# A conditioned convolution block on one core: conditioning and gate computed along the free axis of VectorE

## Chip, core and metric

One core of a Trainium2 chip. The metric is the device time of one execution, in microseconds (us). Three runs of the kernel before took 1729.15, 1729.73 and 1729.89 us; the median is 1729.73.

## What is computed

The block is a decoder layer (width 4096, 256 tokens, batch 1, all f32), cut here to what matters:

```
mod   = silu(c) @ W_ada + b_ada            # c: 4096 values; W_ada: 4096 x 12288
shift, scale, gate = split(mod, 3)         # 4096 values each
h     = rmsnorm(x, norm_g) * (1 + scale) + shift
P     = h @ W_in                           # 4096 x 14336
y_A   = a_b * conv3(a_c * a_x) * silu(a_z)             # mixer A, 2048 channels
y_B   = silu(LN(conv31(b_v * sigmoid(b_g)))) * silu(b_z)  # mixer B, 2048 channels
x     = x + gate * ([y_A, y_B] @ W_out)    # 4096 x 4096
out   = rmsnorm(x, final_g)
```

`W_ada` is 201 MB of the 517 MB that are read: two thirds of it (shift and scale) must be worked out before the rows of `W_in` that they belong to, one third (gate) is needed only in the output projection.

## The kernel before, in words

**Products.** TensorE works through *steps*. A step is one 512 KB load of weights (two contraction tiles of 128 rows by 512 columns): ScalarE rounds it to a high part `w_h` (line 143), VectorE subtracts to get the low part `w_l` (line 144), and TensorE runs 12 products of 512 columns (lines 156 to 158: two contraction tiles, two token tiles, three pairs of parts). `SEGS` (line 59) orders 448 steps of the input projection in six blocks of the contraction (4, 4, 4, 6, 6 and 8 tiles); within a block all 28 column tiles pass, and at the end of each (a *segment*) VectorE adds the PSUM tile to `acc` (line 469). The output projection takes 128 more steps, numbers 448 to 575. The last block begins at step 336.

**Conditioning.** `cact` holds silu(c) with contraction rows on the partitions. Shift and scale of a group of two or four tiles (`mod_steps`, line 176) come from 16 or 32 loads of 512 KB; VectorE multiplies each row of weights by its own scalar and adds it to an accumulator `modacc` (`ada_cols`, line 170), 512 or 1024 columns wide. At the end TensorE sums `modacc` over the partitions with products of one column (line 197), VectorE adds the bias (line 200) and forms `gscT` (line 201). `make_h` (line 255) then scales `x.T` and splits it into `hT`, which the products need.

**Gate.** Four pieces of 1024 columns, 32 loads each (`gate_steps`, line 207). Pieces 0 and 1 run on TensorE, four narrow products side by side per two loads (`step_t`, line 223, products at line 231); pieces 2 and 3 on VectorE (`step_v`, line 218). Each ends in products with a matrix of ones (line 248) that sum over the partitions and leave the gate in all of them. `GATE_RUN` (line 39) spreads the pieces over steps 0 to 70, 70 to 115, 115 to 185 and 185 to 231 counted from step 336.

**Order.** Background work stands in a queue with due steps; `next_w` (line 431) loads and splits the weights of the next step, then runs what is due (`run_due`). The framework's scheduler then fixes one order per engine. All the loads named here go through SP's queue in order, and all of them share the pool `raws` of 10 buffers (line 94): a load goes out when a buffer is free. The parts `w_h` and `w_l` have three buffers each.

**Work of mixer B.** From about step 355 to step 491 the width-31 convolution runs beside the products: per tap four multiplications on ScalarE (line 370) and one addition on VectorE (line 371), 120 taps in all; then a layernorm.

**Start.** `x_stats` (line 274) loads `x.T` in eight pieces and sums squares with products against ones (line 290), while the first 16 loads of conditioning arrive.

Of the kernel before, what the change touches and what calls it, by code (L numbers as in the profile page):

```python
# [55 lines left out]
PK = O_LNB + NB  # L56
# [23 lines left out]
UNITS = [[0, KD]]   # contraction tiles conditioned together: the first, their number  # L80
for _k in range(KD, KT, KD):
    if UNITS[1:] and UNITS[-1][1] == KD and FIRST_USE[_k] - FIRST_USE[_k - KD] < 4:
        UNITS[-1][1] += KD
    else:
        UNITS.append([_k, KD])


@with_exitstack
def decoder_block(ctx: ExitStack, tc: tile.TileContext, x, c, w_mod, w_gate, w_in, w_out, xt, pk, b_gate, final_g, out):
# [3 lines left out]
    ada = ctx.enter_context(tc.tile_pool(name="ada", bufs=1))  # L93
    raws = ctx.enter_context(tc.tile_pool(name="raws", bufs=10))
# [13 lines left out]
    # ---------------- constants and small parameters  # L108
# [38 lines left out]
    def products(ps, act, parts, k0, first, last, tokens=range(NS)):  # L147
        """act[k // 2][:, k % 2, hi/lo, s] is stationary; ps [P, NS, CT]."""
# [11 lines left out]
    def split_act(dst, src):  # L160
        """dst [P, 2, hi/lo, S] <- src [P, 2, S]"""
# [3 lines left out]
    # ---------------- conditioning: silu(c) @ w_ada, 1024 columns at a time  # L165
    modT = const.tile([P, 64], F32, name="modT")
    gscT = const.tile([P, KT], F32, name="gscT")
    hT = {}

    def ada_cols(acc, raw, j):  # L170
        if j == 0:
            nc.vector.tensor_scalar(out=acc, in0=raw, scalar1=cact[:, 0:1], scalar2=None, op0=ALU.mult)
        else:
            nc.vector.scalar_tensor_tensor(out=acc, in0=raw, scalar=cact[:, j:j + 1], in1=acc, op0=ALU.mult, op1=ALU.add)  # L174

    def mod_steps(k0, n):
        """Shift and scale of contraction tiles k0 .. k0 + n."""
        state = {}

        m = 4 // n      # contraction rows per load  # L180
        at = UNITS.index([k0, n])
        first_load = sum(KT * u // 4 for _, u in UNITS[:at])

        def step(j):
            raw = rawt(f"mod{k0}_{j}", (P, m, n * 256))
            nc.sync.dma_start(raw, w_mod[first_load + j // m].rearrange("p (m c) -> p m c", m=m))
            if j == 0:
                state["acc"] = ada.tile([P, n * 256], F32, tag="acc", name=f"modacc{k0}")
            for i in range(m):
                ada_cols(state["acc"], raw[:, i], j + i)  # L190

        def finish():
            acc = state["acc"].rearrange("p (q t c) -> p q t c", t=2, c=256)
            ps = misc(f"modps{k0}", (P, 2, n))
# [3 lines left out]
            for t in range(2):  # L198
                col = 32 * t + k0
                nc.vector.tensor_tensor(out=modT[:, col:col + n], in0=ps[:, t], in1=pks[:, O_BADA + col:O_BADA + col + n], op=ALU.add)  # L200
            nc.vector.scalar_tensor_tensor(out=gscT[:, k0:k0 + n], in0=modT[:, 32 + k0:32 + k0 + n], scalar=1.0, in1=pks[:, O_G + k0:O_G + k0 + n], op0=ALU.add, op1=ALU.mult)

        return [lambda j=j: step(j) for j in range(0, KT, m)] + [finish]
# [70 lines left out]
    def x_stats():  # L274
        """1 / rms of the rows of x, in all partitions"""
        ps = misc("x_ps", (P, S))
        for ci in range(8):
# [355 lines left out]
```

## Time and profile before

| | |
|---|---|
| three runs | 1729.15, 1729.73, 1729.89 us (median 1729.73) |
| span of the profiled execution | 1728.9 us, 21319 instructions |
| TensorE (PE) busy | 1669.5 us, 97% |
| weight loads (PEld), overlapping PE | 1340.1 us, 78% |
| VectorE (DVE) busy | 1506.9 us, 87% |
| ScalarE (ACT) busy | 937.0 us, 54% |
| GpSimd (POOL) busy | 2.9 us |
| DMA | 522.42 MB, mean 302 GB/s, 85.8% of 16 engines for SP's queue |

The span runs from the first to the last instruction of one profiled execution. Its own device time is not given apart from the span; the median of the runs is 0.8 us above the span, and that is what lies around it. Busy times are shares of the whole span and average over stages with different limits; the stages are the start (to 101 us, step 16), the first five blocks (101 to 988 us, steps 16 to 336), the last block with the output projection of mixer A (988 to 1535 us, steps 336 to 512) and the rest.

### The profile page before, as it was taken

To read this page: it belongs to the slowest core of one execution; us is meant where nothing else is said; L and a number is where in the kernel's file an instruction comes from. 1 tells how busy PE (TensorE), PEld (TensorE's weight loads), DVE (VectorE), ACT (ScalarE), POOL (GpSimd) and SP (SyncE) were. 2 spreads that over 40 slices of the span, in tenths; PEclk is the share of its full clock that TensorE was granted. 3 is DMA by queue.
4 is the path that set the end of the run, shared out by engine and by line. 5 is a ranking of instruction groups with operands and counts; after the bars stand their busy time and mean duration, and the time that the engine had idled before them with its cause. 6 is when DMAs were issued, how large, how long until landed. Compare 5 with 4: busy or idle time off the path is not lost.

```text
span 1728.9 us, 21319 instructions
## 1 busy us (share of the span) xinstructions
PE 1669.5 (97%) x7480; PEld 1340.1 (78%) x7480; DVE 1506.9 (87%) x1490; ACT 937.0 (54%) x1304; POOL 2.9 (0%) x10
## 2 busy tenths in 40 slices
PE   2899999999999999999999999999999999999997
PEld 1778788888888888888888877777777887878885
DVE  7887998899898988898898857898998999989996
ACT  3555443443334333343333468888887888564443
POOL 0000000000000000000000000000000000000000
PEclk8899999999999999999999999999999999999998
DMA  9899899999999998999899977766888888779993
GB/s 387 327 317 331 300 344 327 325 320 332 310 335 326 330 326 302 312 352 329 292 340 321 327 243 248 253 230 232 288 278 281 277 286 280 266 254 335 361 345 116
DMA packets 145715, 522.42 MB, mean 302 GB/s; under 512 B 16196, under 2 KB 16196, under 8 KB 145608
## 3 DMA queue, kind: packets, MB, share of 16 engines
q1 hardware_dynamic: 145464, 520.71, 85.8%
q8 instruction: 58, 0.95, 0.2%
q10 hardware_dynamic: 144, 0.35, 0.1%
q14 instruction: 49, 0.40, 0.1%
HBM read 516.81 MB, written 4.19 MB: 301 GB/s over the span
## 4 chain that ended last, share of the span: by engine, by line
PE 86%; DVE 6%; DMA 4%; issue 3%; ACT 1%; SPq 0%; DVEq 0%; ACTq 0%
PE ps L156 23%; PE ps L157 23%; PE ps L158 23%; PE pb L158 3%; PE pb L156 3%; PE pb L157 3%; DVE w_l L144 2%; PE gateps L231 2%; DMA gate<-in_w_gate 2%; DVE cv L371 1%; PE pa L157 1%; PE pa L158 1%; DVE modacc L174 1%; PE pa L156 1%; DMA mod<-in_w_mod 1%
## 5 line engine op out<-in xcount | busy, mean ns | idle before, releaser
L143 ACT CAST w_h<-w_r 128x1024 fp32r<-128x1024 f32 x576 | 603.7, 1052 | 654.2 <-PE ps L158 490.4
L144 DVE TENSOR_TENSOR w_l<-w_r,w_h 128x1024 fp32r<-128x1024 f32 x576 | 700.8, 1220 | 118.8 <-ACT w_h L143 113.2
L156 PE MATMUL ps<-w_h,hT 128*128 128x512 f32 x1792 | 705.8, 394 | 3.0 <-ACT hT L162 2.6
L157 PE MATMUL ps<-w_l,hT 128*128 128x512 f32 x1792 | 700.7, 391 | 5.6 <-DVE w_l L144 5.6
L158 PE MATMUL ps<-w_h,hT 128*128 128x512 f32 x1792 | 699.4, 390 | 0.0
L156 PEld LDWEIGHTS ps<-w_h,hT 128*128 128x128 f32 x1792 | 337.5, 188 | 96.8 <-issue 10.8
L157 PEld LDWEIGHTS ps<-w_l,hT 128*128 128x128 f32 x1792 | 337.5, 188 | 79.9 <-DVE w_l L144 10.9
L158 PEld LDWEIGHTS ps<-w_h,hT 128*128 128x128 f32 x1792 | 337.3, 188 | 70.6
L174 DVE SCALAR_TENSOR_TENSOR modacc<-mod,cact,modacc 128x512 f32<-128x512 f32 (+1 forms) x341 | 337.4, 990 | 4.6 <-DMA mod<-in_w_mod 1.5
L370 ACT ACTIVATE pr<-uT,pks 128x255 f32<-128x255 f32 (+14 forms) x480 | 198.1, 487 | 2.1 <-DVE cv L371 1.6
L469 DVE TENSOR_TENSOR acc<-ps,acc 128x1024 f32<-128x1024 f32 x135 | 164.9, 1221 | 22.9 <-PE ps L158 22.4
L371 DVE TENSOR_TENSOR cv<-cv,pr 128x1020 f32<-128x1020 f32 (+14 forms) x120 | 138.7, 1156 | 27.1 <-ACT pr L370 26.4
L157 PE MATMUL pa<-w_l,yT 128*128 128x512 f32 x256 | 100.6, 393 | 2.4 <-DVE w_l L144 2.4
L156 PE MATMUL pa<-w_h,yT 128*128 128x512 f32 x256 | 100.1, 391 | 0.0
L156 PE MATMUL pb<-w_h,yT 128*128 128x512 f32 x256 | 100.1, 391 | 0.0
L158 PE MATMUL pb<-w_h,yT 128*128 128x512 f32 x256 | 100.0, 391 | 0.0
L158 PE MATMUL pa<-w_h,yT 128*128 128x512 f32 x256 | 100.0, 390 | 0.0
L157 PE MATMUL pb<-w_l,yT 128*128 128x512 f32 x256 | 99.6, 389 | 0.0
L174 DVE SCALAR_TENSOR_TENSOR gateacc<-gate,cact,gateacc 128x1024 f32<-128x1024 f32 x62 | 79.4, 1280 | 5.8 <-DMA gate<-in_w_gate 5.6
L157 PEld LDWEIGHTS pa<-w_l,yT 128*128 128x128 f32 x256 | 48.0, 188 | 14.6 <-DVE w_l L144 4.8
L467 ACT COPY acc<-ps 128x1024 f32<-128x1024 f32 x28 | 28.5, 1017 | 51.7 <-PE ps L158 51.7
L156 PEld LDWEIGHTS pb<-w_h,yT 128*128 128x128 f32 x256 | 48.1, 188 | 10.3 <-ACT w_h L143 0.2
(129 smaller groups left out, 645.2 us busy)
## 6 DMA issues: line engine op xcount, KB each, us to landing
w_r<-in_w_in SPq DMA_DIRECT2D x448, 512.0 KB, 5.2
mod<-in_w_mod SPq DMA_DIRECT2D x256, 512.0 KB, 5.1
gate<-in_w_gate SPq DMA_DIRECT2D x128, 512.0 KB, 4.8
w_r<-in_w_out SPq DMA_DIRECT2D x128, 512.0 KB, 5.1
xs<-in_xt SPq DMA_DIRECT2D x8, 512.0 KB, 10.2
xr<-in_x SPq DMA_DIRECT2D x8, 512.0 KB, 7.0
out<-o SPq DMA_DIRECT2D x16, 256.0 KB, 2.7
xc<-in_xt SPq DMA_DIRECT2D x4, 512.0 KB, 5.2
```

What stands on the lines that cost most here:

```text
L143: nc.scalar.copy(hi, raw)
L144: nc.vector.tensor_tensor(out=lo, in0=raw, in1=hi.bitcast(F32), op=ALU.subtract)
L156: nc.tensor.matmul(out, ah, hi[:, i], start=f, stop=False)
L157: nc.tensor.matmul(out, ah, lo[:, i], start=False, stop=False)
L158: nc.tensor.matmul(out, al, hi[:, i], start=False, stop=l)
L174: nc.vector.scalar_tensor_tensor(out=acc, in0=raw, scalar=cact[:, j:j + 1], in1=acc, op0=ALU.mult, op1=ALU.add)
L231: nc.tensor.matmul(state["ps"][r:r + 1, 0], cact[:, j + i:j + i + 1], raws_[i][:, h * CT:(h + 1) * CT], start=j == 0, stop=j == KT - 2)
L370: nc.scalar.activation(out=pr[:, j, sh:], in_=u[:, j, :S - sh], func=AF.Copy, scale=cbw[:, 4 * i + j, TAPS - 1 - sh:TAPS - sh])
L371: nc.vector.tensor_tensor(out=o[:, :, sh:], in0=o[:, :, sh:], in1=pr[:, :, sh:], op=ALU.add)
L467: nc.scalar.copy(acc[e], ps)
L469: nc.vector.tensor_tensor(out=acc[e], in0=ps, in1=acc[e], op=ALU.add)
```

## The change

The layout of `W_ada` is turned: one *output column* per partition, the contraction along the free axis. silu(c) then has to stand in all partitions: `broadcast_c` loads c in four rows of 1024, TensorE copies each to 128 partitions (two products with one contraction row each), ScalarE applies silu into `cB` (128 x 4096). One `tensor_tensor_reduce` on VectorE multiplies a load of 128 columns by 1024 contraction rows with `cB` and sums along the free axis, starting from the bias or from the sum before; four of them make 128 columns. In the engine's order it is two instructions: the sum of products (128x1024) and one that writes the sum (128x1). Shift and scale are thereby done without TensorE; the unit of work is one tile, 8 loads and 8 such pairs, and `gscT`. All of the gate, 128 loads, is done the same way on VectorE, over steps 0 to 170 from step 336; the 4096 gate values are then transposed, written to DRAM and read back into all partitions, 1024 columns at a time, where the final weights are loaded. The loads keep their number and size (384 of 512 KB). `raws` has 7 buffers in place of 10 (`cB` takes 16 KB of each partition). `x_stats` now adds all eight pieces on VectorE before four products, and is called before the first conditioning; the weights of the first two steps are loaded ahead of the last four pieces of first work. The due steps of shift and scale follow the same rule, for one tile at a time.

```diff
-GATE_PE = (0, 1)    # gate columns (1024 each) worked out on TensorE, the others on VectorE
-GATE_RUN = {0: (0, 70), 1: (70, 115), 2: (115, 185), 3: (185, 231)}  # when, in steps from the last block on
+ROW = 1024
+GATE_RUN = (0, 170)
...
-    raws = ctx.enter_context(tc.tile_pool(name="raws", bufs=10))
+    raws = ctx.enter_context(tc.tile_pool(name="raws", bufs=7))
...
-    def ada_cols(acc, raw, j):
-        if j == 0:
-            nc.vector.tensor_scalar(out=acc, in0=raw, scalar1=cact[:, 0:1], scalar2=None, op0=ALU.mult)
-        else:
-            nc.vector.scalar_tensor_tensor(out=acc, in0=raw, scalar=cact[:, j:j + 1], in1=acc, op0=ALU.mult, op1=ALU.add)
+    def broadcast_c():
+
+        for q in range(D // ROW):
+            row = bigt(f"crow{q}", (P, ROW))
+            nc.sync.dma_start(row[:1], c[:, q * ROW:(q + 1) * ROW])
+            ps = pmm.tile([P, NS, CT], F32, tag="ps", name=f"cps{q}")
+            for h in range(2):
+                nc.tensor.matmul(ps[:, h], ones[:1], row[:1, h * CT:(h + 1) * CT], start=True, stop=True)
+            nc.scalar.activation(out=cB[:, q * ROW:(q + 1) * ROW], in_=ps, func=AF.Silu)
+
+    def ada_steps(name, srcs, bias, dst):
...
+        def step(q):
+            raw = rawt(f"{name}_{q}", (P, ROW))
+            nc.sync.dma_start(raw, srcs[q])
+            if q == 0:
+                state["part"] = part.tile([P, 4], F32, tag="part", name=f"part{name}")
+            p = state["part"]
+            nc.vector.tensor_tensor_reduce(out=raw, in0=raw, in1=cB[:, q * ROW:(q + 1) * ROW], scale=1.0, scalar=p[:, q - 1:q] if q else bias, op0=ALU.mult, op1=ALU.add, accum_out=dst if q == D // ROW - 1 else p[:, q:q + 1])
...
-            for t in range(2):
-                for i in range(n):
-                    nc.tensor.matmul(ps[:, t, i:i + 1], acc[:, i // 2, t, (i % 2) * P:(i % 2 + 1) * P], ones[:, 0:1], start=True, stop=True)
...
-                    nc.tensor.matmul(state["ps"][r:r + 1, 0], cact[:, j + i:j + i + 1], raws_[i][:, h * CT:(h + 1) * CT], start=j == 0, stop=j == KT - 2)
...
+    def gate_finish():
+
+        ps = misc("gate_ps", (P, P))
+        nc.tensor.transpose(ps[:KT], gateT, ident)
+        row = rawt("gate_row", (P, P))
+        nc.scalar.copy(row[:KT], ps[:KT])
+        nc.sync.dma_start(gate_d.rearrange("(k p) -> k p", p=P), row[:KT])
+
+    def gate_steps():
+        work = [f for k in range(KT) for f in ada_steps(f"gate{k}", w_gate[k], pks[:, O_BGATE + k:O_BGATE + k + 1], gateT[:, k:k + 1])]
+        return work + [gate_finish]
...
+    broadcast_c()
+    rstd = x_stats()
+    first_steps = [f for k in range(KD) for f in mod_steps(k)]
+    for f in first_steps[:-4]:
         f()
-    rstd = x_stats()
-    for f in first_steps[2:]:
+    load_ahead(AHEAD)
+    for f in first_steps[-4:]:
         f()
...
+    spread(gate_steps(), start_last + GATE_RUN[0], start_last + GATE_RUN[1])
...
+            t = gate[dt // 2] = bigt(f"gate{dt // 2}", (P, 1024))
+            nc.sync.dma_start(t, gate_d[dt * CT:dt * CT + 1024].partition_broadcast(P))
```

Two places of the order move as follows. The first is VectorE's queue in the last block, from the split of step 356 to that of step 358 (names carry buffer numbers; `w356_l` is the low part of step 356's weights, `cv0` and `pr0` are the convolution's sum and one tap's products, `acc18` a segment's sum). Before:

```order
L144 TENSOR_TENSOR w356_l_8088<-w356_r_8085,w356_h_8087 128x1024
L371 TENSOR_TENSOR cv0_7779<-cv0_7779,pr0_7_8011 128x4x249
L144 TENSOR_TENSOR w357_l_8108<-w357_r_8105,w357_h_8107 128x1024
L469 TENSOR_TENSOR acc18_1112<-ps24_18_8004,acc18_1112 128x1024
L371 TENSOR_TENSOR cv0_7779<-cv0_7779,pr0_8_8035 128x4x248
L144 TENSOR_TENSOR w358_l_8132<-w358_r_8129,w358_h_8131 128x1024
```

Now:

```order
L138 TENSOR_TENSOR w356_l_8000<-w356_r_7997,w356_h_7999 128x1024
L186 ISA gate4_0_8003,partgate4_8005<-gate4_0_8003,cB_95,pks_90 128x1024
L186 ISA partgate4_8005 128x1
L348 TENSOR_TENSOR cv0_7689<-cv0_7689,pr0_8_7952 128x4x248
L437 TENSOR_TENSOR acc18_1073<-ps24_18_7918,acc18_1073 128x1024
L138 TENSOR_TENSOR w357_l_8024<-w357_r_8021,w357_h_8023 128x1024
L348 TENSOR_TENSOR cv0_7689<-cv0_7689,pr0_9_7979 128x4x247
L186 ISA gate4_1_8033,partgate4_8005<-gate4_1_8033,cB_95,partgate4_8005 128x1024
L186 ISA partgate4_8005 128x1
L138 TENSOR_TENSOR w358_l_8051<-w358_r_8048,w358_h_8050 128x1024
```

Two pairs of the gate (rows of L186) stand between the splits of two steps, where before only the convolution and the segment's sum stood; the gate's products of that time were in TensorE's queue.

The second is SP's queue at the end of the gate, in the layernorm of mixer B (`w504_r` is the load of step 504's weights, `gate31_3` the last load of the gate, `gate_d` the write of the gate to DRAM). Before:

```order
L138 DMA w503_r_12044<-in_w_out 128x1024
L215 DMA gate2_25_12050<-in_w_gate 128x1024
L138 DMA w504_r_12070<-in_w_out 128x1024
L138 DMA w505_r_12109<-in_w_out 128x1024
L215 DMA gate2_26_12115<-in_w_gate 128x1024
L138 DMA w506_r_12130<-in_w_out 128x1024
```

Now:

```order
L182 DMA gate31_3_11992<-in_w_gate 128x1024
L132 DMA w503_r_12007<-in_w_out 128x1024
L132 DMA w504_r_12035<-in_w_out 128x1024
L210 DMA gate_d_96<-gate_row_12020 32x128
L132 DMA w505_r_12074<-in_w_out 128x1024
L132 DMA w506_r_12092<-in_w_out 128x1024
```

The write of the gate stands ahead of the load for step 505. It needs the last pair on VectorE, then a transpose on TensorE that stands behind the products of the layernorm's variance, then a copy on ScalarE.

## Rows read from the trace of the kernel before

**Rows 1.** The page: the chain that ended last, by engine, then by line.

```profile
PE 86%; DVE 6%; DMA 4%; issue 3%; ACT 1%; SPq 0%; DVEq 0%; ACTq 0%
PE ps L156 23%; PE ps L157 23%; PE ps L158 23%; PE pb L158 3%; PE pb L156 3%; PE pb L157 3%; DVE w_l L144 2%; PE gateps L231 2%; DMA gate<-in_w_gate 2%; DVE cv L371 1%; PE pa L157 1%; PE pa L158 1%; DVE modacc L174 1%; PE pa L156 1%; DMA mod<-in_w_mod 1%
```

**Rows 2.** Busy time of each engine by stage of the span (columns in the first row).

```profile
core 0: us, PE busy (x) PEld busy (x) DVE busy (x) ACT busy (x) POOL busy (x), PEclk, DMA share, GB/s
0.00:101.00 101.00, 60.09 (x230) 47.60 (x231) 79.98 (x109) 46.23 (x51) 0.99 (x8) 0.85 0.94 354
101.00:988.00 887.00, 883.83 (x3937) 729.15 (x3937) 790.82 (x757) 369.39 (x371) 0.00 (x0) 1.00 0.92 323
988.00:1535.00 547.00, 544.28 (x2523) 414.95 (x2522) 473.02 (x463) 434.60 (x772) 1.91 (x2) 1.00 0.77 261
1535.00:1728.90 193.90, 181.30 (x795) 148.41 (x793) 163.03 (x163) 86.78 (x113) 0.00 (x0) 0.97 0.81 296
```

**Rows 3.** Groups of VectorE instructions in the stretch 988 to 1535 us.

```profile
L174 DVE SCALAR_TENSOR_TENSOR gateacc<-gate,cact,gateacc 128x1024 f32<-128x1024 f32 x30 | 38.4, 1281 | 5.7 <-DMA gate<-in_w_gate 5.6
...
L172 DVE TENSOR_SCALAR gateacc<-gate,cact 128x1024 f32<-128x1024 f32 x1 | 0.7, 747 | 0.0
```

**Rows 4.** Groups of the whole span by shape: costs that the sums use.

```profile
L174 DVE SCALAR_TENSOR_TENSOR modacc<-mod,cact,modacc 128x1024 f32<-128x1024 f32 x155 | 198.3, 1279 | 0.1
...
L231 PE MATMUL gateps<-gate,cact 128*1 128x512 f32 x256 | 36.3, 591 | 0.0
...
L248 PE MATMUL gatesum<-gateacc,ones 128*128 128x512 f32 x16 | 7.5, 592 | 0.0
...
L172 DVE TENSOR_SCALAR modacc<-mod,cact 128x1024 f32<-128x1024 f32 x5 | 3.7, 747 | 0.0
...
L524 ACT ACTIVATION_READ_ACCUMULATOR xr<-o 128x1 f32 x14 | 2.6, 185 | 0.0
```

**Rows 5.** VectorE's timeline around 611, 1430 and 1719 us.

```profile
610.72 1.28 DVE L174 SCALAR_TENSOR_TENSOR modacc<-mod,cact,modacc 128x1024 f32<-128x1024 f32 x1
611.91 1.22 DVE L469 TENSOR_TENSOR acc<-ps,acc 128x1024 f32<-128x1024 f32 x1
...
1430.03 2.35 DVE L144 TENSOR_TENSOR w_l<-w_r,w_h 128x1024 fp32r<-128x1024 f32 x2
...
1719.34 0.15 DVE L585 TENSOR_SCALAR o_v<-o_v 128x1 f32<-128x1 f32 x1
```

**Rows 6.** Timeline of the start: first conditioning, a statistics product, first product.

```profile
5.53 0.49 DVE L172 TENSOR_SCALAR modacc<-mod,cact 128x512 f32<-128x512 f32 x1 [5.53 <-DMA mod<-in_w_mod]
...
22.36 3.56 PE L290 MATMUL x_ps<-xq,ones 128*128 128x256 f32 x8 [3.83 <-DVE xq L288]
...
50.78 0.79 PE L156 MATMUL ps<-w_h,hT 128*128 128x512 f32 x1 [2.62 <-ACT hT L162]
```

**Rows 7.** Busy time in 43.2 us of the middle, sixteen steps (columns as in Rows 2).

```profile
388.80:432.00 43.20, 43.20 (x192) 35.79 (x191) 41.56 (x36) 16.57 (x17) 0.00 (x0) 1.00 0.95 332
```

**Rows 8.** TensorE's conditioning products in the stretch 101 to 988 us.

```profile
L197 PE MATMUL modps<-ones,modacc 128*128 128x1 f32 x96 | 11.1, 243 | 0.0
```

**Rows 9.** VectorE's conditioning in the same stretch.

```profile
L174 DVE SCALAR_TENSOR_TENSOR modacc<-mod,cact,modacc 128x1024 f32<-128x1024 f32 (+1 forms) x276 | 288.8, 1046 | 1.8
...
L172 DVE TENSOR_SCALAR modacc<-mod,cact 128x1024 f32<-128x1024 f32 (+1 forms) x8 | 5.2, 647 | 0.0
```

**Rows 10.** DMA issues: bytes of each, median us from issue to landing.

```profile
w_r<-in_w_in SPq DMA_DIRECT2D x448, 512.0 KB, 5.2
```

**Rows 11.** Two stretches where TensorE paused (columns as in Rows 2).

```profile
190.00:213.00 23.00, 20.96 (x88) 15.69 (x87) 23.00 (x27) 7.34 (x7) 0.00 (x0) 1.00 0.81 264
86.40:129.60 43.20, 40.66 (x174) 32.49 (x173) 34.60 (x43) 22.30 (x24) 0.00 (x0) 0.96 0.91 317
```

**Rows 12.** TensorE's timeline just after its first product.

```profile
51.37 0.63 PE L157 MATMUL ps<-w_l,hT 128*128 128x512 f32 x1
51.80 0.63 PE L156 MATMUL ps<-w_h,hT 128*128 128x512 f32 x1
```

More of the change, by code (lines that the diff above doesn't have):

```diff
@@ L55 @@
 O_LNB = O_LNG + NB
-PK = O_LNB + NB
+O_BGATE = O_LNB + NB
+PK = O_BGATE + KT
 def _segments():
@@ L79, with decoder_block @@
     FIRST_USE.setdefault(_k, _t)
[L80 to L83, printed above, removed]
-    else:
-        UNITS.append([_k, KD])
 @with_exitstack
-def decoder_block(ctx: ExitStack, tc: tile.TileContext, x, c, w_mod, w_gate, w_in, w_out, xt, pk, b_gate, final_g, out):
+def decoder_block(ctx: ExitStack, tc: tile.TileContext, x, c, w_mod, w_gate, w_in, w_out, xt, pk, final_g, out):
     nc = tc.nc
@@ L92, in decoder_block @@
     big = ctx.enter_context(tc.tile_pool(name="big", bufs=33))
-    ada = ctx.enter_context(tc.tile_pool(name="ada", bufs=1))
-    raws = ctx.enter_context(tc.tile_pool(name="raws", bufs=10))
+    cbc = ctx.enter_context(tc.tile_pool(name="cbc", bufs=1))
+    part = ctx.enter_context(tc.tile_pool(name="part", bufs=4))
+    dram = ctx.enter_context(tc.tile_pool(name="dram", bufs=1, space=bass.MemoryType.DRAM))
+    raws = ctx.enter_context(tc.tile_pool(name="raws", bufs=7))
     split = ctx.enter_context(tc.tile_pool(name="split", bufs=3))
@@ L167, in decoder_block @@
     gscT = const.tile([P, KT], F32, name="gscT")
+    gateT = const.tile([P, KT], F32, name="gateT")
+    cB = cbc.tile([P, D], F32, name="cB")
     hT = {}
-    def ada_cols(acc, raw, j):
-        if j == 0:
-            nc.vector.tensor_scalar(out=acc, in0=raw, scalar1=cact[:, 0:1], scalar2=None, op0=ALU.mult)
-        else:
-            nc.vector.scalar_tensor_tensor(out=acc, in0=raw, scalar=cact[:, j:j + 1], in1=acc, op0=ALU.mult, op1=ALU.add)
-    def mod_steps(k0, n):
-        state = {}
[L180 to L190, printed above, removed]
-        def finish():
-            acc = state["acc"].rearrange("p (q t c) -> p q t c", t=2, c=256)
-            ps = misc(f"modps{k0}", (P, 2, n))
-            for t in range(2):
-                for i in range(n):
-                    nc.tensor.matmul(ps[:, t, i:i + 1], acc[:, i // 2, t, (i % 2) * P:(i % 2 + 1) * P], ones[:, 0:1], start=True, stop=True)
[L198 to L203, printed above, removed]
@@ new lines, in broadcast_c @@
+    def broadcast_c():
[7 more added lines that the diff above has]
+    def ada_steps(name, srcs, bias, dst):
+        state = {}
+        def step(q):
[5 more added lines that the diff above has]
+            nc.vector.tensor_tensor_reduce(out=raw, in0=raw, in1=cB[:, q * ROW:(q + 1) * ROW], scale=1.0, scalar=p[:, q - 1:q] if q else bias, op0=ALU.mult, op1=ALU.add, accum_out=dst if q == D // ROW - 1 else p[:, q:q + 1])
+        return [lambda q=q: step(q) for q in range(D // ROW)]
@@ new lines, in mod_steps @@
+    def mod_steps(k):
+        def finish():
+            nc.vector.scalar_tensor_tensor(out=gscT[:, k:k + 1], in0=modT[:, 32 + k:33 + k], scalar=1.0, in1=pks[:, O_G + k:O_G + k + 1], op0=ALU.add, op1=ALU.mult)
+        work = []
+        for t in (1, 0):
+            col = 32 * t + k
+            work += ada_steps(f"mod{k}_{t}", w_mod[k, t], pks[:, O_BADA + col:O_BADA + col + 1], modT[:, col:col + 1])
+        return work + [finish]
+    gate_d = dram.tile([D], F32, name="gate_d")
+    gate = {}
@@ new lines, in gate_finish @@
+    def gate_finish():
[7 more added lines that the diff above has]
+        return work + [gate_finish]
+    plan = [(w_in[e], k) for _, e, k0, k1 in SEGS for k in range(k0, k1, KD)]
@@ new lines, in decoder_block, with load_ahead @@
+    end_in = len(plan)
+    start_last = sum((k1 - k0) // KD for b, _, k0, k1 in SEGS if b < len(BLOCKS) - 1)
+    conv_end = end_in + CONV_END
+    plan += [(w_out[dt], k0 + k) for k0 in (0, KT // 2) for dt in range(NDT) for k in range(0, KT // 2, KD)]
+    loaded = []
+    step = 0
+    def load_ahead(last):
+        while len(loaded) <= min(last, len(plan) - 1):
+            src, k = plan[len(loaded)]
+            loaded.append(load_w(src, k, f"w{len(loaded)}", 0 <= len(loaded) - len(plan) + KT // 2 // KD < HOLD))
@@ L284, in x_stats @@
             nc.scalar.activation(out=sq, in_=xc, func=AF.Square)
-            if ci % 2 == 0:
+            if ci == 0:
                 total = sq
-                continue
-            nc.vector.tensor_tensor(out=total, in0=total, in1=sq, op=ALU.add)
-            for i in range(4):
-                nc.tensor.matmul(ps, ones, total[:, i], start=ci + i == 1, stop=ci + i == 10)
+            else:
+                nc.vector.tensor_tensor(out=total, in0=total, in1=sq, op=ALU.add)
+        for i in range(4):
+            nc.tensor.matmul(ps, ones, total[:, i], start=i == 0, stop=i == 3)
         y = const.tile([P, S], F32, name="x_rstd")
@@ L420, in gate_B @@
             split_act(t, o[:, 2 * h:2 * h + 2])
-    plan = [(w_in[e], k) for _, e, k0, k1 in SEGS for k in range(k0, k1, KD)]
-    end_in = len(plan)
-    start_last = sum((k1 - k0) // KD for b, _, k0, k1 in SEGS if b < len(BLOCKS) - 1)
-    conv_end = end_in + CONV_END
-    plan += [(w_out[dt], k0 + k) for k0 in (0, KT // 2) for dt in range(NDT) for k in range(0, KT // 2, KD)]
-    loaded = []
-    step = 0
     def next_w():
-        while len(loaded) <= min(step + AHEAD, len(plan) - 1):
-            src, k = plan[len(loaded)]
-            loaded.append(load_w(src, k, f"w{len(loaded)}", 0 <= len(loaded) - len(plan) + KT // 2 // KD < HOLD))
+        load_ahead(step + AHEAD)
         parts = loaded[step]
@@ L441, in decoder_block @@
     hull = [(0, KD)]
-    need = [(max(FIRST_USE[k] - LEAD, 1), k + n) for k, n in UNITS[1:]]
+    need = [(max(FIRST_USE[k] - LEAD, 1), k + KD) for k in range(KD, KT, KD)]
     while hull[-1][1] < KT:
@@ L448, in due @@
         return float(np.interp(done, [n for _, n in hull], [t for t, _ in hull]))
-    for k, n in UNITS[1:]:
-        work = mod_steps(k, n)
-        queue.extend((due(k + n * (j + 1) / len(work)), f) for j, f in enumerate(work))
-        queue.append((max(due(k + n) + 0.01, FIRST_USE[k] - LEAD + 0.02), lambda k=k, n=n: make_h(k, n)))
-    for ci, (t0, t1) in GATE_RUN.items():
-        spread(gate_steps(ci), start_last + t0, start_last + t1)
+    for k in range(KD, KT):
+        work = mod_steps(k)
+        queue.extend((due(k + (j + 1) / len(work)), f) for j, f in enumerate(work))
+        if k % KD == KD - 1:
+            n = k + 1 - KD
+            queue.append((max(due(k + 1) + 0.01, FIRST_USE[n] - LEAD + 0.02), lambda n=n: make_h(n, KD)))
+    spread(gate_steps(), start_last + GATE_RUN[0], start_last + GATE_RUN[1])
     acc = {}
```

55 lines of the change are left out of this document (4 added, 51 removed).

## Prediction, made before the changed kernel was run

> **What bounds the kernel now.** I read the chain first: 86% of the span lies on TensorE, nearly all of it products, and the gate's narrow products (L231) have 2% of it [rows 1]. Then the stages, since one share for all of them hides where VectorE is full [rows 2]. From 101 to 988 us (320 steps) TensorE is busy for 883.8 of 887.0 us and VectorE for 790.8. From 988 to 1535 us (176 steps) TensorE is busy for 544.3 of 547.0, VectorE for 473.0. So TensorE ends every wait in both stages, but VectorE has only 11 to 14% of slack, and it is the engine that this change loads. A step costs TensorE 2.70 us: 43.2 us hold 192 products, which is 16 steps [rows 7]. The 176 steps would then need 475 us, and they take 547: the rest is work beside the products, the gate's above all.
>
> **What a pair costs on VectorE.** The new instruction is not in this trace, so I bound it. Its nearest row multiplies and adds two f32 operands of 128x1024 with one scalar per partition: 1.28 us [rows 4]. On the queue such an instruction starts the next one after 1.19 us (610.72 to 611.91), since neighbours overlap by some 0.09; two splits take 2.35, not twice 1.22 [rows 5]. The write of the sum is a 128x1 instruction. The smallest one on VectorE lasts 0.15 [rows 5]; ScalarE's read of its accumulator, the same kind of step on another engine, 0.185 [rows 4]. With and without overlap a pair costs 1.19 + 0.07 = 1.26 to 1.28 + 0.19 = 1.47. I take 1.20 + 0.16 = **1.36 us**, because the sum must be complete before it is written, which leaves the overlap to the first of the two.
>
> [...] I go by the row, because the sum differs from it only in the write of one value per partition.
>
> **The stage from 988 to 1535 us, steps 336 to 512.** Removed from VectorE: 30 + 1 accumulations of the gate, 38.4 + 0.7 = 39 us [rows 3], which leaves 473 - 39 = 434. Added: the order has 127 pairs between the splits of steps 336 and 512 (nearly all of the gate: GATE_RUN ends at step 506), 127 x 1.36 = 173. Sum 607 us on an engine that works in order. TensorE drops the gate's products (36.3 us, [rows 4]) and needs little over 475. So VectorE becomes the bound by about 100 us, and the stage takes its 607 us: **+60** against 547. Two corrections are left out as equal: a full queue overlaps neighbours more often than a queue with gaps does (up to 10 us off), and VectorE will still wait now and then (2% is 12 us on). That a full VectorE need hardly wait at all is in the trace: from 190 to 213 us it is busy for 23.00 of 23.00 us while TensorE pauses [rows 11]. What covered the gate before was TensorE's time and VectorE's gaps; both are used up, and the products are late next, each step waiting for its `w_l`.
>
> **From 101 to 988 us.** TensorE loses the partition sums of shift and scale, 11.1 us [rows 8], all on its path. VectorE exchanges 288.8 + 5.2 = 294 us [rows 9] for 223 pairs, 223 x 1.36 = 303, so 800 of about 876 us: still not the bound. **-11** (bounds: -15 with the waits for VectorE that these sums brought, +10 if the shorter reserve of buffers is felt).
>
> **The start.** Before, the first accumulation runs at 5.5 us and the first product at 50.8 [rows 6]. Now VectorE's first pairs need `cB`, for which TensorE makes eight products of 512 columns. Its products of 256 columns take 3.56 us for four (eight records, two each) at this time [rows 6], so these take about 8 x 1.78 = 14 us, and the last quarter of `cB` is there at some 19 us. VectorE's sums: 34 pairs before the 16th split, 46 us, against 68 accumulations of half the width, about as long. Three more additions for the statistics, fewer products in between. **+3** (0 to +8).
>
> **The write of the gate.** SP issues in order, and the load for step 505 stands behind the write, which waits for the last pair, the variance's products and a copy. A load needs 5.2 us to land [rows 10]; VectorE has a part of the layernorm to do meanwhile. **+4** (0 to +10). The loads back, 14 steps later, have at least eight steps of room and cost nothing; without that room each would cost its landing, 5 us.
>
> **From 1535 us on.** VectorE loses 35 accumulations, which TensorE's products hid. TensorE loses half of the products with ones (7.5 us in all, [rows 4]): **-4** (-6 to 0).
>
> **Sum.** Span 1728.9 and 0.8 around it: 1729.7, which is the median of the runs. 3 - 11 + 60 + 4 - 4 = +52: **1782 us**. A measurement of this kernel can tell 0.2%, about 3.5 us, from no change.
>
> **Rivals.**
>
> *VectorE keeps up (faster).* The change frees TensorE of 36 + 11 + 7 us; if a pair were cheap, that gain would stay. The other terms sum to -8, so the stage may take 555 us before the change costs anything: a pair of (555 - 434) / 127 = 0.95 us decides. One kind of 128x1024 instruction on VectorE is that fast: one source and a scalar, 0.747 us [rows 4]. At 0.75 + 0.07 = 0.82 the stage takes 434 + 104 = 538, -9, and the whole 1729.7 - 9 - 8 = **1713**. Against it: every row with two f32 tensors takes 1.22 or more. Chance 0.05.
>
> [...] Chance 0.05.
>
> *Seven buffers are too few.* From 101 to 988 us some 540 loads come (323 GB/s x 887 us in pieces of 0.524 MB, [rows 2]), 0.61 per us; ten buffers mean 16.4 us from issue to release, seven 11.5, of which 5.2 is landing [rows 10]. It decides where a load must lie longer than the 6.3 us that are left. If they need 6.7, seven buffers pass 0.588 loads per us, the stage takes 918 us, +31 in place of -11: **1824**. For it: DMA is at 0.92 there [rows 2]. Against: ten buffers leave 11.2 us of lying, and VectorE's idle time in that stage is nearly all put down to other engines (1.8 us before its conditioning, [rows 9]). Chance 0.10.
>
> *TensorE's clock falls.* With VectorE the bound, TensorE works for about 80% of the stage in short pieces. In one stretch with pauses its clock was 0.96, in another, busy 91%, 1.00 [rows 11]. [...] Chance 0.06.
>
> **How the numbers follow.** The forecast has 0.74. Its own bounds: low, pairs at 1.26, tighter packing, no losses elsewhere: 434 - 10 + 160 = 584 (+37), with 0 - 15 + 0 - 6 gives 1746; high, pairs at 1.47 and waits of 4%: (434 + 187) x 1.04 = 646 (+99), with 8 + 10 + 10 - 2 gives 1855. Few of these come together, so I take 1752 to 1838, which holds the third rival too; left out are the first two rivals, most of the fourth and the forecast's ends, some 0.2. Faster 0.05 (the first rival), same 0.02 (its border), slower 0.93.
>
> **What would show it.** Right: between steps 336 and 512 VectorE busy over 95% and TensorE near 80%; TensorE's waits on `w_l` (L138) first in its list; 384 sums of 1.2 to 1.3 us and 384 writes of 0.15 to 0.19; the stage before shorter by 5 to 15 us. Wrong: sums well under 1 us or over 2; VectorE waiting for DMA before 988 us; a clock under 0.95 in the last block; the loss lying in the start.

## The result: 1793.5 us, 3.7% slower

The changed kernel takes 1793.45 us (median of 4 runs, 1792.71 to 1794.99), the kernel before in the same session 1729.81 (4 runs, 1729.15 to 1730.38): ratio 1.0369, 95% interval 1.0354 to 1.0384. That lies in the range of the prediction and 11 us above its forecast. The stages show that this is two misses that partly cancel: the price of a pair on VectorE was too high, and TensorE's products became slower, which no term had.

The chain of waits of the changed kernel, by engine and by line, answers to [rows 1]: TensorE falls from 86% to 58%, VectorE rises from 6% to 25%.

```profile
PE 58%; DVE 25%; issue 9%; DMA 4%; ACT 3%; DVEq 0%; ACTq 0%
PE ps L151 15%; PE ps L152 15%; PE ps L150 15%; DVE w_l L138 7%; DVE cv L348 6%; DVE gate L186 5%; PE pb L150 3%; PE pb L152 3%; PE pb L151 3%; DMA mod<-in_w_mod 3%; DVE acc L437 2%; DVE mod L186 2%; ACT w_h L137 1%; ACT pr L347 1%; PE cps L173 1%
```

The windows by stage of the changed kernel (columns as in [rows 2]); the borders are the starts of the `w_l` of steps 16, 336 and 512, as in the stages of before:

```profile
99.50:1001.60 902.10, 897.77 (x3849) 723.56 (x3848) 785.54 (x922) 367.51 (x369) 0.00 (x0) 1.00 0.91 318
1001.60:1597.10 595.50, 535.66 (x2231) 406.56 (x2230) 582.99 (x688) 429.14 (x762) 0.00 (x0) 0.99 0.81 271
1597.10:1793.20 196.10, 183.50 (x796) 148.66 (x794) 124.75 (x128) 84.42 (x109) 0.00 (x0) 0.98 0.66 221
```

Read them one by one against [rows 2]. From step 336 to 512 VectorE is busy for 583 of 595 us, and the stage is 49 us longer: that is the forecast's mechanism. But the stage before it, where TensorE is busy for 898 of 902 us and VectorE has over 110 us to spare, is also 15 us longer, though TensorE has less to do there. That was not forecast.

The same contrast in the longest waits of the changed kernel between steps 336 and 512 (line, line waited for, us, times, longest): the weight loads and the products wait for `w_l` (69.6 and 41.6 us; the two rows overlap in time, TensorE is idle for 60 us of this stage), and VectorE itself waits for next to nothing.

```profile
PEld ps L151 <- DVE w_l L138: 69.6, 69, 2.5
...
PE ps L151 <- DVE w_l L138: 41.6, 54, 2.1
...
DVE w_l L138 <- ACT w_h L137: 4.9, 6, 2.4
```

**What a pair costs.** VectorE's timeline of the changed kernel, from 1299.80 us on (start, us, engine and line, operation):

```profile
1299.80 1.28 DVE L186 CUSTOM_DVE_ANT_0 gate<-gate,cB,partgate 128x1024 f32<-128x1024 f32 x1
1301.00 0.09 DVE L186 DVE_READ_ACCUMULATOR2_ANT partgate<- 128x1 f32 x1
1301.00 0.42 DVE L318 TENSOR_TENSOR yfA<-yfA,psA 128x256 f32<-128x256 f32 x1
...
1307.24 1.28 DVE L186 CUSTOM_DVE_ANT_0 gate<-gate,cB,partgate 128x1024 f32<-128x1024 f32 x1
1308.44 0.09 DVE L186 DVE_READ_ACCUMULATOR2_ANT partgate<- 128x1 f32 x1
1308.44 0.42 DVE L318 TENSOR_TENSOR yfA<-yfA,psA 128x256 f32<-128x256 f32 x1
```

The sum takes 1.28 us, as the row that the prediction took for it [rows 4]. The write of its result takes 0.09, and the next instruction starts at the same moment as that write: on its queue a pair costs 1.20 us, not 1.36. An instruction that reads the sum starts later: in the first conditioning the next sum of the same tile starts behind the write, 1.32 us after the one before it.

```profile
19.42 1.28 DVE L186 CUSTOM_DVE_ANT_0 mod<-mod,cB,partmod 128x1024 f32<-128x1024 f32 x1
20.62 0.08 DVE L186 DVE_READ_ACCUMULATOR2_ANT partmod<- 128x1 f32 x1
20.74 1.28 DVE L186 CUSTOM_DVE_ANT_0 mod<-mod,cB,partmod 128x1024 f32<-128x1024 f32 x1
```

**TensorE's pace.** Take 43.2 us in the middle of either kernel's second stage, at full clock and with TensorE busy throughout. [Rows 7] have 192 products in them; the changed kernel has 187, with less on VectorE and on DMA. (Such a count takes in products that an end of the stretch cuts, so it is good to one or so: in the very stretch of the next line the kernel before has 193.)

```profile
400.00:443.20 43.20, 43.20 (x187) 35.05 (x186) 39.90 (x47) 16.84 (x16) 0.00 (x0) 1.00 0.92 319
```

and behind step 512, where no sums run any more, TensorE's timeline of the changed kernel:

```profile
1659.65 0.39 PE L151 MATMUL pb<-w_l,yT 128*128 128x512 f32 x1
1659.88 0.39 PE L152 MATMUL pb<-w_h,yT 128*128 128x512 f32 x1
1660.11 0.40 PE L150 MATMUL pb<-w_h,yT 128*128 128x512 f32 x1
1660.34 0.40 PE L151 MATMUL pb<-w_l,yT 128*128 128x512 f32 x1
1660.58 0.40 PE L152 MATMUL pb<-w_h,yT 128*128 128x512 f32 x1
...
1661.96 0.40 PE L152 MATMUL pb<-w_h,yT 128*128 128x512 f32 x1
```

Ten products from 1659.65 to 1661.96 are 0.231 us each. At the same work the kernel before has 0.226, ten from 1599.68 to 1601.94:

```profile
1599.68 0.39 PE L157 MATMUL pb<-w_l,yT 128*128 128x512 f32 x1
...
1601.94 0.39 PE L158 MATMUL pb<-w_h,yT 128*128 128x512 f32 x1
```

Sixteen steps without any wait take 44.6 us here (2.79 each) and 43.5 in the kernel before (2.72). Some 0.07 us in each of 320 steps is more than the whole gain forecast for that stage. Nothing in the diff touches a product. What did change is where the tiles lie: the new constants shift `hT` and `yT` by 128 bytes, and the four partial sums shift the weights by 128 more (from 96 past a multiple of 2048 for all of them to 224 and 352).

### The profile page after: what moved, and what is told of

Same layout as the page of the kernel before. It is cut to its first block, busy times and chain, and to the rows that moved or that the text cites. A ratio compares the mean times of both kernels' runs of the same rounds, so it can differ in the third digit from the quotient of the medians.

```text
span 1793.2 us, 20728 instructions
## 1 busy us (share of the span) xinstructions
PE 1679.6 (94%) x7073; PEld 1320.8 (74%) x7073; DVE 1571.1 (88%) x1842; ACT 930.6 (52%) x1292; POOL 1.0 (0%) x8
## 4 chain that ended last, share of the span: by engine, by line
PE 58%; DVE 25%; issue 9%; DMA 4%; ACT 3%; DVEq 0%; ACTq 0%
PE ps L151 15%; PE ps L152 15%; PE ps L150 15%; DVE w_l L138 7%; DVE cv L348 6%; DVE gate L186 5%; PE pb L150 3%; PE pb L152 3%; PE pb L151 3%; DMA mod<-in_w_mod 3%; DVE acc L437 2%; DVE mod L186 2%; ACT w_h L137 1%; ACT pr L347 1%; PE cps L173 1%
## 5 line engine op out<-in xcount | busy, mean ns | idle before, releaser
L151 PE MATMUL ps<-w_l,hT 128*128 128x512 f32 x1792 | 718.3, 401 | 48.3 <-DVE w_l L138 47.6
L186 DVE CUSTOM_DVE_ANT_0 mod<-mod,cB,partmod 128x1024 f32<-128x1024 f32 x192 | 245.7, 1279 | 17.7 <-DMA mod<-in_w_mod 16.8
L186 DVE CUSTOM_DVE_ANT_0 gate<-gate,cB,partgate 128x1024 f32<-128x1024 f32 x96 | 123.2, 1284 | 0.6 <-DMA gate<-in_w_gate 0.5
L151 PE MATMUL pa<-w_l,yT 128*128 128x512 f32 x256 | 104.7, 409 | 7.0 <-DVE w_l L138 6.6
L186 DVE CUSTOM_DVE_ANT_0 mod<-mod,cB,pks 128x1024 f32<-128x1024 f32 x64 | 81.9, 1280 | 14.0 <-DMA xs<-in_xt 9.2
L150 PEld LDWEIGHTS pa<-w_h,yT 128*128 128x128 f32 x256 | 48.7, 190 | 13.7 <-ACT w_h L137 2.2
```

The costliest lines, as they stand in the source:

```text
L150: nc.tensor.matmul(out, ah, hi[:, i], start=f, stop=False)
L151: nc.tensor.matmul(out, ah, lo[:, i], start=False, stop=False)
L186: nc.vector.tensor_tensor_reduce(out=raw, in0=raw, in1=cB[:, q * ROW:(q + 1) * ROW], scale=1.0, scalar=p[:, q - 1:q] if q else bias, op0=A ...
```

## Experiments: where the operands of the products lie

All times are medians; each ratio is to the kernel before, run on the same chip. Offsets are the address of a tile within a partition, modulo 2048. The first two experiments swap the places between the kernels and leave the order of the instructions alone.

**Places put back in the changed kernel.**

```diff
-    part = ctx.enter_context(tc.tile_pool(name="part", bufs=4))
...
     split = ctx.enter_context(tc.tile_pool(name="split", bufs=3))
+    part = ctx.enter_context(tc.tile_pool(name="part", bufs=4))
+    tail = ctx.enter_context(tc.tile_pool(name="tail", bufs=1))
...
-    gateT = const.tile([P, KT], F32, name="gateT")
+    gateT = tail.tile([P, KT], F32, name="gateT")
```

> The changed kernel with the four partial sums and the gate's column put behind all other tiles, so that the operands of the products (hT, yT, w_h, w_l) lie at the same offsets as in the kernel before (96 bytes past a multiple of 2048; in the changed kernel 224 for hT and yT, 352 for the split weights); no instruction is moved. Theory P (places): the products of the changed kernel are slower because of where their operands lie. Then the spacing of products comes back from 0.233 to 0.227 us, a step from 2.79 to 2.71, steps 16 to 336 from 902 to some 877 us, and the whole to 1758 to 1768 us. Theory V (VectorE): the slower pace comes with the new work on the other engines. Then 1790 to 1796 us and a step of 2.79 us.

Measured: 1770.99 us, ratio 1.0239 (1.0224 to 1.0254): 22.5 us of the loss are gone. The same 43.2 us hold 192 products again, and the stages are

```profile
400.00:443.20 43.20, 43.20 (x192) 35.77 (x191) 41.16 (x48) 16.89 (x16) 0.00 (x0) 1.00 0.92 321
...
100.40:985.50 885.10, 877.88 (x3849) 720.48 (x3848) 783.72 (x922) 368.45 (x369) 0.00 (x0) 1.00 0.93 324
985.50:1577.80 592.30, 527.30 (x2231) 403.81 (x2230) 582.71 (x689) 428.69 (x762) 0.00 (x0) 0.99 0.81 272
1577.80:1769.50 191.70, 179.13 (x795) 148.07 (x793) 124.62 (x128) 84.67 (x109) 0.00 (x0) 0.98 0.68 226
```

The first stage loses 17 us and the last 4, where TensorE sets the pace; the one in the middle, where VectorE does, only 3. The total is 3 us above what theory P expected: the first stage takes 885 us in place of 877 (the part on buffers comes back to this).

**Places moved in the kernel before.**

```diff
+    gap = ctx.enter_context(tc.tile_pool(name="gap", bufs=1))
     raws = ctx.enter_context(tc.tile_pool(name="raws", bufs=10))
...
+    nc.gpsimd.memset(const.tile([P, 32], F32, name="pad0"), 0.0)
+    nc.gpsimd.memset(gap.tile([P, 32], F32, name="pad1"), 0.0)
     cact = const.tile([P, KT], F32, name="cact")
```

> The kernel before with 128 bytes put ahead of hT and yT, and 128 more ahead of the weights, so that both lie where the changed kernel has them; no instruction on TensorE, VectorE or ScalarE is changed. Theory P: a step takes 2.79 instead of 2.71 us, steps 16 to 336 some 912 instead of 887 us, the whole 1760 to 1775 us. Theory V: 1728 to 1732 us.

Measured: 1763.96 us, ratio 1.0200 (1.0185 to 1.0216). 34 us from 256 bytes that nobody reads. Its 43.2 us hold 187 products:

```profile
400.00:443.20 43.20, 43.20 (x187) 35.05 (x186) 40.34 (x35) 15.82 (x16) 0.00 (x0) 1.00 0.93 322
```

**Which place counts.** Five more kernels differ from the kernel before only in the size of `pad0` (ahead of `hT` and `yT`, it moves the weights along) or of `pad1` (ahead of the weights alone); the one with 64 bytes, for instance, is

```diff
+    gap = ctx.enter_context(tc.tile_pool(name="gap", bufs=1))
...
+    nc.gpsimd.memset(gap.tile([P, 16], F32, name="pad1"), 0.0)
```

> The kernel before with 32 bytes put ahead of hT and yT: they and the weights all lie 128 bytes past a multiple of 2048 instead of 96. Theory R (relation): products are slow when the stationary tile and the moving tile lie at different offsets; here they lie at the same one, so 1728 to 1732 us. Theory O (offset of a tile itself): the time may change either way; a shorter step than 2.71 us, down to 2.6, would be a gain for both kernels (1665 to 1720 us).

> The kernel before with 128 bytes put ahead of the weights alone: hT and yT stay at 96 past a multiple of 2048, the split weights lie at 224. Theory R: as slow as with both moved apart, a step of 2.79 us and 1760 to 1770 us. Theory O, in the form that the place of hT and yT counts: 1728 to 1732 us.

> The kernel before with 128 bytes put ahead of hT and yT, which moves the weights along: all lie at 224 past a multiple of 2048. Theory R: 1728 to 1732 us, a step of 2.71 us. Theory O, in the form that the place of hT and yT counts: 1760 to 1770 us, a step of 2.79 us.

> The kernel before with 1024 bytes put ahead of the weights alone, so that they lie 1024 bytes further into a stretch of 2048 than hT and yT. If any distance makes the products slow: 1760 to 1770 us. If the distance counts by what is left of it after multiples of 512 (the width of one stationary tile) or of 1024: 1728 to 1732 us.

> The kernel before with 64 bytes put ahead of the weights alone. If any distance makes the products slow by the same amount, as 128 did: 1760 to 1770 us. If the loss grows with the distance: some 1745 us. If a distance under 128 costs nothing: 1728 to 1732 us.

| pad0, pad1 (bytes) | `hT`, `yT` at | weights at | apart | us | ratio, 95% interval |
|---|---|---|---|---|---|
| 32, 0 | 128 | 128 | 0 | 1730.15 | 0.9997 (0.9988 to 1.0007) |
| 128, 0 | 224 | 224 | 0 | 1730.85 | 0.9999 (0.9990 to 1.0009) |
| 0, 1024 | 96 | 1120 | 1024 | 1730.41 | 1.0000 (0.9991 to 1.0010) |
| 0, 64 | 96 | 160 | 64 | 1743.49 | 1.0078 (1.0063 to 1.0094) |
| 0, 128 | 96 | 224 | 128 | 1762.78 | 1.0186 (1.0171 to 1.0202) |
| 128, 128 | 224 | 352 | 128 | 1763.96 | 1.0200 (1.0185 to 1.0216) |

The rows of 0, 128 and of 0, 64, in this order, for the same 43.2 us:

```profile
400.00:443.20 43.20, 43.20 (x187) 35.04 (x186) 40.55 (x35) 15.89 (x16) 0.00 (x0) 1.00 0.93 322
```

```profile
400.00:443.20 43.20, 43.20 (x191) 35.44 (x190) 41.09 (x36) 16.38 (x16) 0.00 (x0) 1.00 0.94 330
```

Theory R holds: neither offset matters by itself, what counts is how far the stationary tile (`hT`, `yT`) and the moving one (the weights) are apart. 64 bytes cost 13 us, 128 cost 32 to 34, 1024 nothing.

Two things limit this. A product reads a slice of 512 bytes of the stationary tile, which begins 0, 512, 1024 or 1536 bytes into a stretch of 2048 (two token tiles, two parts). So the kernel before already has these four distances, all at the same pace (from 200 to 900 us nine tenths of the spacings from one start to the next are 226 or 227 ns), and 1024 bytes more give it the same four again: what was tried is 0, 64 and 128 bytes beyond a multiple of 512, and nothing else. And the buffers of the raw loads (`raws`) moved along with `w_h` and `w_l` in every run; TensorE reads the split weights alone, but no run parts the two.

Why the distance counts stays open: no wait or queue shows it, only a slower pace. With 64 bytes not every product has it. From 200 to 900 us the median from one start to the next is 232 ns from the high part's product to the low part's (lines 158 to 159 there), 226 from that to the third product (line 160) and 229 from the third to the next first; the kernel before has 227 for all three, with 128 bytes it is 232 for all three.

## Experiments: VectorE's load and the buffers

**The gate's sums and their loads left out.**

```diff
-        work = [f for k in range(KT) for f in ada_steps(f"gate{k}", w_gate[k], pks[:, O_BGATE + k:O_BGATE + k + 1], gateT[:, k:k + 1])]
-        return work + [gate_finish]
+        nc.gpsimd.memset(gateT, 0.5)
+        return [gate_finish]
...
-    spread(gate_steps(), start_last + GATE_RUN[0], start_last + GATE_RUN[1])
+    spread(gate_steps(), start_last + GATE_RUN[1], start_last + GATE_RUN[1] + 1)
```

> The changed kernel without the loads and the sums of the gate (the gate is the constant 0.5); its write and its loads back stay. If VectorE is what bounds steps 336 to 512 with its 127 pairs, the stage falls from 595 us to what the products need at the pace of this kernel, 176 x 2.79 = 491 us, and the whole to 1683 to 1695 us, with TensorE busy for over 98% of that stage. If the loss of that stage were the pace of the products or another wait, at most some 50 us would go: 1740 us or more.

Measured: 1715.20 us, ratio 0.9917 (0.9903 to 0.9932), between the two expectations. The stage from step 336 to 512, the changed kernel's 595 us, is now

```profile
1001.60:1516.00 514.40, 507.35 (x2233) 408.38 (x2232) 440.04 (x433) 428.61 (x761) 0.00 (x0) 1.00 0.59 184
```

TensorE is busy for 98.6% of it, and without the pairs the stage is 81 us shorter. The 128 loads are gone as well, so this run alone does not part VectorE's work from the loads; the next two, which keep every load, do. VectorE's busy time falls by 583 - 440 = 143 us for 127 pairs, 1.13 each in busy time. Not right was the floor: TensorE needs 507 us, since the stage also holds products that are no steps (those of the two mixers, some 15 us), which 176 x 2.79 = 491 leaves out.

**The gate in four pieces, the last of them behind step 512.** The changed kernel with the places put back, and:

```diff
-GATE_RUN = (0, 170)
+GATE_RUN = {0: (0, 62), 1: (62, 124), 2: (124, 182), 3: (182, 222)}
...
-    gate_d = dram.tile([D], F32, name="gate_d")
+    gate_d = [dram.tile([ROW], F32, name=f"gate_d{ci}") for ci in range(4)]
```

> The changed kernel with the places put back, and the gate written in four pieces of 1024 values, each with its own transpose, copy and write, so that its sums may run until step 558 (62, 62, 58 and 40 steps for a piece) where they now end at 506. About 93 pairs are then left between steps 336 and 512 in place of 127. If VectorE is the bound of that stage, at 1.36 us for a pair, it takes some 46 us less than the 592 us it takes with the places put back alone, and the 35 pairs that move behind step 512 (48 us) fit beside the products there, where VectorE was busy for 27 of 40 us: 1722 to 1735 us in place of 1771. If they don't fit there: 1750 us or more.

Measured: 1754.68 us, ratio 1.0131 (1.0113 to 1.0150). The two stages:

```profile
985.00:1543.00 558.00, 518.36 (x2237) 411.61 (x2237) 543.70 (x620) 428.64 (x762) 0.00 (x0) 0.98 0.78 260
1543.00:1722.00 179.00, 170.71 (x712) 135.94 (x711) 148.63 (x163) 76.13 (x95) 0.00 (x0) 0.97 0.83 308
```

The first expectation missed. The stage has 94 pairs in place of 127 and is 34 us shorter where 46 were expected, 1.03 us for a pair, with VectorE still at 97%: its load sets the time. But from step 512 to the end the kernel takes 210 us instead of 192, so half of that is given back. VectorE has room there (149 of 179 us); the loads are late instead, as the wait of ScalarE's copies shows (28.7 us from 1543 to 1722; with the gate in one piece, 4.8 us from 1578 to 1736):

```profile
ACT w_h L138 <- DMA w_r<-in_w_out: 28.7, 19, 4.2
```

That these waits make up all of the 18 us is not shown. Some of it is TensorE's clock, which is lower for 7 and for 3 us there (from 1606 and from 1657 us): on average it is 0.91 from 1600 to 1640 us and 0.97 from 1640 to 1690, with the gate in one piece 1.00 in both.

**Half of the gate back on TensorE.** Columns 0 and 1 as in the kernel before, 2 and 3 as sums; places put back.

```diff
+GATE_RUN = {0: (0, 85), 1: (85, 170), 2: (0, 85), 3: (85, 170)}
...
+        spread((gate_steps_pe if ci < 2 else gate_steps)(ci), start_last + t0, start_last + t1)
```

> One part of the change undone: the changed kernel with the places put back, in which two of the gate's four columns are worked out on TensorE again, as in the kernel before, beside the two that stay sums on VectorE (64 pairs, written in two pieces), both within 170 steps from step 336 on. On its queue VectorE starts the instruction behind a pair after 1.20 us, and its other work in that stage is 434 us: 434 + 64 x 1.20 = 511 us and some 12 of waits; TensorE has 505 + 36 = 541 us. So TensorE is the bound again, the stage takes 540 to 550 us in place of 592, and the whole 1716 to 1728 us, some 45 to 50 less than with the places put back alone and no more than the kernel before. If the loss of that stage is not VectorE's load but the seven buffers or the order of the loads, which stay, it takes over 570 us: 1745 us or more.

Measured: 1738.31 us, ratio 1.0061 (1.0037 to 1.0085). All the loads are there, and the stage is 31 us shorter than the 592 of the run with the places put back. TensorE is busy for 98% of it, so the bound is back there, and VectorE's 510 us are the 511 that were expected:

```profile
985.00:1545.00 560.00, 551.19 (x2488) 409.75 (x2487) 510.01 (x560) 434.51 (x775) 1.91 (x2) 1.00 0.82 286
```

That takes 33 us off the changed kernel with the places put back, 12 fewer than expected at least. TensorE is busy for 551 us, 10 more than was reckoned, and 7 more than in the kernel before [rows 2]; it waits for the loads of its gate, too (its products 3.6 us, its weight loads 7.8). This is the fastest that was tried with sums and the whole gate, and it does not beat the kernel before.

**Buffers.** Seven in the kernel before, and six in the changed kernel with the places put back:

```diff
-    raws = ctx.enter_context(tc.tile_pool(name="raws", bufs=10))
+    raws = ctx.enter_context(tc.tile_pool(name="raws", bufs=7))
```

> The kernel before with seven buffers for loads in place of ten. By the prediction's third rival (seven buffers are too few) the stage from step 16 to 336 becomes longer by some 31 us or more: 1750 to 1770 us. By the forecast it loses at most some waits: 1730 to 1738 us.

```diff
-    raws = ctx.enter_context(tc.tile_pool(name="raws", bufs=7))
+    raws = ctx.enter_context(tc.tile_pool(name="raws", bufs=6))
```

> The changed kernel with the places put back and six buffers for loads in place of seven. With seven, VectorE's sums waited 24.4 us for their loads from step 16 to 336 (26 times), and that stage took 885 us where the prediction's terms make 876. If what is missing of the gain there is the shorter reserve of buffers, one buffer less makes it worse: waits of 35 us or more, the stage 890 to 905 us, the whole 1776 to 1795 us. If the buffers are not felt, and the sums wait only because they are early: 1768 to 1774 us, the stage 883 to 887.

Measured: 1738.78 us with seven in the kernel before, ratio 1.0052 (1.0035 to 1.0069); of the 8.5 us that its span grows, 1 is lost from step 16 to 336, 3.5 from there to 512 and 5.6 behind it (the start gives some back). With six in the changed kernel with the places put back 1783.99 us, 13 more than with seven, 10 of them from step 16 to 336 (895 us). VectorE's wait for the conditioning's loads in that stage doubles, and the weight loads and the products wait more for `w_l`; the waits of that stage with seven buffers, then with six:

```profile
DVE mod L187 <- DMA mod<-in_w_mod: 24.4, 26, 1.9
...
PEld ps L152 <- DVE w_l L139: 15.0, 19, 1.4
...
PE ps L152 <- DVE w_l L139: 7.1, 16, 1.0
```

```profile
DVE mod L187 <- DMA mod<-in_w_mod: 48.2, 47, 2.9
...
PEld ps L152 <- DVE w_l L139: 21.3, 24, 1.4
...
PE ps L152 <- DVE w_l L139: 11.5, 20, 1.0
```

So the third rival's mechanism exists and is small: seven buffers are at the edge.

## Why the forecast came out near, term by term

Differences from the kernel before, in us. The borders are the starts of `w_l` before rounding (100.98, 988.06 and 1534.60 us in the kernel before), so a row can differ by some tenths from the windows shown. The write of the gate holds up the load of step 505, so its +4 stands in the stage from 336 to 512.

| from step to step | forecast | changed kernel | with the places put back |
|---|---|---|---|
| start to 16 | +3 | -1.5 | -0.6 |
| 16 to 336 | -11 | +15.0 | -2.1 |
| 336 to 512 | +60 + 4 = +64 | +48.9 | +45.8 |
| 512 to the end | -4 | +1.8 | -2.6 |
| sum | +52 | +64.3 | +40.6 |

That the whole came within 11 us is in part luck. With the places put back, the change that the forecast reckoned with takes 1771 us, 11 less than forecast; the places, which no term had, add 22.5 and put it 11 above.

**The mechanism was right.** VectorE becomes the bound from step 336 to 512, busy for 97.9%, and the products wait for `w_l`. Leaving the gate out, thinning it and giving half of it back to TensorE all move that stage the way its pairs say. Of the signs of being right, VectorE's share, the wait for `w_l` and the 384 sums of 1.2 to 1.3 us came true; the writes are shorter (0.08 to 0.10 us in place of 0.15 to 0.19), TensorE is busier, and the stage before became longer.

**The step "I take 1.20 + 0.16 = 1.36 us" was too dear.** The write does not hold the queue up, because the instruction behind it starts along with it (both at 1301.00 us, 1.20 behind the sum's start); the reason given, that the sum must be complete first, holds for a reader of the value (1.32 us) and not for the next instruction in line. With 1.20 the stage is 434 + 127 x 1.20 = 586, and the 12 us in which VectorE is not busy make 598 (measured 595.5). Those 12 us are the 2% that the prediction named and set against closer packing; 4 of them lie in the 19 us around the write of the gate.

**"It needs little over 475" was too low**, though it did not enter the sum. Without any gate TensorE is busy for 507 us, and the rows at hand gave about as much: 544.3 less the gate's 36.3 is 508 [rows 2, rows 4]. The forecast of 80% for TensorE was low (536 of 595, 90%), in part for the same reason.

**The stage from 16 to 336 failed on a term that the prediction did not have.** 17 of the 26 us between -11 and +15 are the places of the operands: 902.1 with them, 885.0 without. The prediction took the product's pace over from the kernel before, as if an unchanged instruction kept its price. The other 9 us lie within the bounds it gave (-15 to +10). Some 4 of them come of the borders alone: without the 96 products of [rows 8] and 8 of the gate, the stage holds 3937 - 104 = 3833 products before and 3849 with the places put back, 16 more of 0.227 us. Most of the rest is waiting: TensorE is idle for 7.2 us there in place of 3.2, and VectorE's sums wait 24.4 us for loads (21.6 in the changed kernel), which the prediction had named as a sign of being wrong. That buffers have a part in it is shown by the run with six; how much is theirs is not.

**The start** came out 4.5 us better than forecast. The products for `cB` end at 16.2 us, as reckoned; the first row is that of TensorE, the second the first sum on VectorE:

```profile
2.25 13.99 PE L173 MATMUL cps<-crow,ones 1*128 1x512 f32 x16 [2.25 <-DMA crow<-in_c]
```

```profile
9.17 1.28 DVE L186 CUSTOM_DVE_ANT_0 mod<-mod,cB,pks 128x1024 f32<-128x1024 f32 x1 [9.17 <-DMA xs<-in_xt]
```

The first product then starts at 52.93 us, 2 later than in [rows 6], and that is made up by step 16. That the cheaper pairs do this is likely but not shown: the granted clock of the start differs too (0.91, 0.85 in [rows 2]), and the same start in the run without the gate's sums ends 1.3 us later.

**The write of the gate** cost what was forecast or a little more. Behind step 512 nothing shows, but the forecast's place for it was the load of step 505. There ScalarE's copy waits 8.6 us for the transpose (line, line waited for, us, times, longest), SP issues nothing from 1556.1 us until the write at 1568.68, and no load moves from 1560 to 1566 us (last two columns):

```profile
ACT gate_row L209 <- PE gate_ps L207: 8.6, 1, 8.6
```

```profile
1568.68 0.32 SPq L210 DMA_DIRECT2D gate_d<-gate_row  x1
```

```profile
1560.00:1566.00 6.00, 5.41 (x24) 4.09 (x23) 6.00 (x7) 0.00 (x0) 0.00 (x0) 1.00 0.00 0
...
1573.50:1578.70 5.20, 4.88 (x12) 3.82 (x13) 5.13 (x8) 1.38 (x2) 0.00 (x0) 0.50 1.02 414
```

From the start of step 503 to that of step 512 the changed kernel takes 38.2 us, 36.8 with the places put back, and the kernel before 29.8. So some 7 us is an estimate of the price, inside the bounds (0 to +10); no run leaves out the write alone. One part was not in the forecast: ScalarE works in order too, and while its copy waits, the rounding of the next weights stands behind it (the one ahead of the copy starts at 1558.71 us, the copy at 1568.40, the next rounding at 1570.29).

**The rivals.** VectorE keeping up fell with the first row of a sum (1.28 us), and so did sums of over 2 us: the longest of the 384 takes 1.30. TensorE's clock is 0.99 on average in the stage from step 336 on, over the 0.95 below which the prediction would have been wrong, so the fourth rival fell, but a lower clock is there. Three times, for 17 us in all, it is at 0.50 (the last row above): from 1012, from 1371 and from 1572 us, each time behind pauses (in the 9 us ahead TensorE is busy for 6.4, 5.3 and 6.7). That the pauses bring it on is not shown. 29 products follow each other at 0.43 us there in place of 0.232, which costs 6 us. Seven buffers are felt, but by 1 us in that rival's stage when the kernel before is given them, where the rival had the stage longer by 31.

## What to carry to other kernels

Where an engine has 11 to 14% of slack, count what moves onto it against that slack stage by stage: here 173 us by the forecast, 152 by the measured price, came in place of 39 onto 74 us of room. Price an accumulating instruction by the start of the next one on its queue (1.20 us here, 1.32 where that one reads the sum), not by its own duration plus that of its write. Where a small result goes through a copy and a write at the end, look at what stands behind the two in their queues. And when a change adds or drops any tile, look at how far apart the operands of the matrix products come to lie: check the pace of a product in a stretch without waits, in both kernels, before giving a reason for the rest.

## What the runs showed that was not expected

Two tiles read by the same product cost time by their distance alone: with the stationary and the moving tile a multiple of 512 bytes apart 43.2 us hold 192 products, with 64 bytes more 191, with 128 bytes more 187, at the same granted clock of 1.00. In a kernel that is bound by its products this is 0.8% and 1.9% of the whole time (1743.49 and 1762.78 against 1730), and no wait, queue or DMA row shows it.
